# A doubling scan over 16 block sums, wider scan operations, a second buffer for the output tables and a new order of the chain's steps

## The chip, the cores and the metric

The kernel runs on one core of one Trainium2 chip. The metric is the device time of one execution in microseconds (us). The five engines of the core run their own queues in order: PE (matmul), DVE (vector), ACT (scalar), POOL (GpSimd) and SP, which here only issues DMAs. ACT issues DMAs too.

## The reference

One layer of a bidirectional hybrid encoder: 2048 tokens of width 1024, all in float32.

```
h = rms_norm(x);  [q | k | v | z_attn | u_ssm | z_ssm | gates] = h @ w_in
attn = windowed_gqa(q, k, v, sink, bias) * silu(z_attn)          # 8 heads, band of +-128
for each of 2 directions:                                        # 32 groups, 64 states each
    bu = u_group @ b_bar                                         # complex
    x[t] = a_bar * x[t-1] + bu[t]     (or backward)              # diagonal complex recurrence
    y += Re(c x)
y = gelu(y); y = y * sigmoid(y @ w_glu + b_glu); ssm = y * silu(z_ssm)
merged = sigmoid(g_attn) * (attn @ w_a) + sigmoid(g_ssm) * (ssm @ w_s)
out = rms_norm(x + merged @ w_out)
```

## The kernel before

Every large matmul is done as three (high part by high part, high by low, low by high), so each operand is split: ACT copies the high part, DVE or POOL subtracts it to get the low part. Weights arrive 128 columns at a time through SP into `raw` (two buffers); ACT writes `wh` (L164), POOL writes `wl` in four pieces (L156).

The program has one main order, a list of projections (`proj`: 24 matmuls of 512 columns into one of three `pj` banks, L221 to L223, then one evacuation by ACT). Beside it runs a side generator, `chain`: first the recurrence (`ssm`), then the attention, then preparations for the tail. After every six matmuls the main order grants the chain some credit (rate 1.237 per twelve matmuls while the recurrence runs), and the chain advances by one `yield` for each whole credit. So a step of the chain is a place in the order of every queue: what it issues stands there between the projections' instructions, on all engines. The order is written out by hand; nothing is moved by a planner, and an engine that waits holds up all that is queued behind it on that engine.

The recurrence works on 32 groups, four at a time (`GB = 4`), in eight rounds. T = 8 tokens are merged into one column, so M = 256 columns are scanned. A round i has these parts:

- `prep_w(i)` and `prep_o(i)`: POOL makes the input tables `wt` and the output tables `wo`, each by 24 TENSOR_TENSORs of 128x128 (L639 to L641).
- `load_u(i)`: four DMAs on SP bring the round's inputs into the tile `u` (one buffer). `split_u(i, half)` makes high and low parts of two groups (ACT `U0h`, `U1h` at L672; DVE `U0l`, `U1l` at L673); after half 1 the next round is loaded.
- `mats(i)`: PE transposes `wt` (L699), ACT and DVE make `Wh`, `Wl` (L702, L693).
- `inject(i)`: PE makes the scan's input (L756), ACT copies it into `X` (L757, L758).
- `zmat(i)`: `sign_o` changes the sign of `wo[1]` on ACT (L655), PE multiplies `wo` (L723, L730), DVE copies to `Z` (L731 to L733), and DMAs reorder it into `M`.
- `split_m(i)`, `split_o(i)`: high and low parts of `M` and of `wo` (`Mh`, `ws0h`, `ws1h` on ACT, `Ml`, `ws0l`, `ws1l` on DVE, all at L672, L673).
- `scan(i)`: all on DVE, in place in `X`: a tree of levels up (n = 128, 64, 32, ... 1 columns to update) and down (1, 3, 7, ... 127). With n > 32 a level is three SCALAR_TENSOR_TENSORs for each of the four groups (L774 to L776); with n up to 32 it is four TENSOR_TENSORs for all four groups at once (L786 to L789). Each call of `fma` yields an estimate of its cost, and a step of the chain (with one piece of `pieces()`) is taken each time the estimates add up to a slot.
- `hcopy(i, half)`: ACT copies two groups of `X` to `Hh` (L806), DVE makes `Hl` (L808), one buffer each. `emit(i, half)`: PE makes the output (L818, L822), ACT evacuates it (L826).

While `scan(i)` runs, `pieces()` of round i does the work of its neighbours: `mats(i+1)`, `emit(i-1)`, `inject(i+1)` and `zmat(i+1)`. `hcopy(i, 0)` comes after the last piece.

Of the kernel before, what the change touches and what calls it, by code (L numbers as in the profile page):

```python
# [7 lines left out]
F32 = mybir.dt.float32  # L8
# [17 lines left out]
GB = 4  # L26
# [12 lines left out]
def kernel(  # L39
# [381 lines left out]
    wo_im = prm.tile([128, G, T], F32, name="wo_im")  # L421
    NLEV = 8
    lv_re = prm.tile([128, G, NLEV], F32, name="lv_re")
    lv_im = prm.tile([128, G, NLEV], F32, name="lv_im")
    lv_ni = prm.tile([128, G, NLEV], F32, name="lv_ni")
    lv_sw = prm.tile([128, G, 2, NLEV], F32, name="lv_sw")
    bx_re = prm.tile([128, G + 1, C], F32, name="bx_re")
    bx_im = prm.tile([128, G + 1, C], F32, name="bx_im")
# [6 lines left out]
    def ssm_params(pool):  # L435
# [50 lines left out]
        def ts(o, a, s1, s2, o1, o2):  # L486
            if s2 is None:
                V.tensor_scalar(o, a, s1, None, o1)
            else:
                V.tensor_scalar(o, a, s1, s2, o1, o2)  # L490
            return o
# [100 lines left out]
            cmul(pw_re[:, :, i], pw_im[:, :, i], pw(i // 2), pw(i - i // 2))  # L592
        yield 8
        V.tensor_copy(lv_re[:, :, 0], pw_re[:, :, T])
        V.tensor_copy(lv_im[:, :, 0], pw_im[:, :, T])
        for i in range(1, NLEV):
            a = (lv_re[:, :, i - 1], lv_im[:, :, i - 1])
            cmul(lv_re[:, :, i], lv_im[:, :, i], a, a)
        ts(lv_ni, lv_im, -1.0, None, ALU.mult, None)
        V.tensor_copy(lv_sw[:, :, 0], lv_ni)  # L600
        V.tensor_copy(lv_sw[:, :, 1], lv_im)
        f, b_ = slice(0, 64), slice(64, 128)
        for dst_i, dst_o, src in ((wi_re, wo_re, pw_re), (wi_im, wo_im, pw_im)):
            V.tensor_copy(dst_i[f], src[f, :, 0:T])
# [16 lines left out]
    def ssm(pool):  # L621
# [9 lines left out]

        def table(i, tag, p_re, p_im, q_re, q_im, bufs):

            tmp = [pool.tile(sh, F32, tag=f"t{n}", name=f"t{n}") for n in range(2)]
            o = [pool.tile(sh, F32, tag=f"{tag}{n}", name=f"{tag}{n}", bufs=bufs) for n in range(2)]
            pr, pi, qr, qi = bc(p_re, i, 1), bc(p_im, i, 1), bc(q_re, i, 0), bc(q_im, i, 0)
            for n, (a, b, c, d, op) in enumerate(((pr, qr, pi, qi, ALU.subtract), (pr, qi, pi, qr, ALU.add))):
                for g in range(GB):
                    Q.tensor_tensor(tmp[0][:, g], a[:, g], b[:, g], ALU.mult)  # L639
                    Q.tensor_tensor(tmp[1][:, g], c[:, g], d[:, g], ALU.mult)  # L640
                    Q.tensor_tensor(o[n][:, g], tmp[0][:, g], tmp[1][:, g], op)  # L641
            return o

        def prep_w(i):
            st[i] = {"wt": table(i, "wt", wi_re, wi_im, bb_re, bb_im, 1)}

        def prep_o(i):
            st[i]["wo"] = table(i, "wo", wo_re, wo_im, cc_re, cc_im, 1)

        def split_o(i):  # L650
            st[i]["ws"] = [split(t, sh, f"ws{n}", 1) for n, t in enumerate(st[i].pop("wo"))]
# [9 lines left out]

            return bass.AP(tensor=t.tensor, offset=t.offset + g * C * T * M, ap=[[M, T], [T * M, C], [1, M]])

        def load_u(i):
            U = pool.tile([128, GB, M], F32, tag="u", name="u")
            for g in range(GB):
                nc.sync.dma_start(out=U[:, g], in_=chan(uS, i * GB + g))
            raw_u[i] = U

        def split(raw, shape, tag, bufs):  # L670
            hi, lo = [pool.tile(shape, F32R, tag=tag + t, name=tag + t, bufs=bufs) for t in "hl"]
# [2 lines left out]
            return hi, lo  # L674

        def split_u(i, half):
            u = raw_u[i][:, half * 2:half * 2 + 2]
            st[i].setdefault("U", []).append(split(u, [128, 2, M], f"U{half}", 2))
            if half == 1 and i + 1 < NB:
                load_u(i + 1)  # L680

        def split_m(i):
            st[i]["M"] = split(st[i].pop("m"), [128, GB, 128], "M", 1)
# [77 lines left out]
        def scan(i):  # L761

            g0 = i * GB
            X = st[i]["X"]

            def fma(dst, src, lev, n):

                if n > 32:
                    for g in range(GB):
                        d, s_ = X[:, g, :, dst], X[:, g, :, src]  # L770
                        re = lv_re[:, g0 + g, lev:lev + 1]
                        im = lv_im[:, g0 + g, lev:lev + 1]
                        ni = lv_ni[:, g0 + g, lev:lev + 1]
                        V.scalar_tensor_tensor(d, s_, re, d, ALU.mult, ALU.add)  # L774
                        V.scalar_tensor_tensor(d[:, 0], s_[:, 1], ni, d[:, 0], ALU.mult, ALU.add)
                        V.scalar_tensor_tensor(d[:, 1], s_[:, 0], im, d[:, 1], ALU.mult, ALU.add)  # L776
                        if g % 2 == 1:
                            yield 1.5 if n > 64 else 0.9
                else:
                    sh = [128, GB, 2, n]  # L780
                    t = pool.tile([128, GB, 2, 32], F32, tag="ft", name="ft", bufs=1)[:, :, :, 0:n]
                    u = pool.tile([128, GB, 2, 32], F32, tag="fu", name="fu", bufs=1)[:, :, :, 0:n]
                    d, s_ = X[:, :, :, dst], X[:, :, :, src]
                    re = lv_re[:, g0:g0 + GB, lev:lev + 1].unsqueeze(2).to_broadcast(sh)
                    sw = lv_sw[:, g0:g0 + GB, :, lev:lev + 1].to_broadcast(sh)
                    V.tensor_tensor(t, s_, re, ALU.mult)  # L786
                    V.tensor_tensor(u, s_[:, :, ::-1], sw, ALU.mult)
                    V.tensor_tensor(t, t, u, ALU.add)
                    V.tensor_tensor(d, d, t, ALU.add)  # L789
                    yield 0.25 + 4 * GB * 2 * n / 960.0  # L790

            for lev in range(NLEV):
                s_ = 1 << lev
                n = M // (2 * s_)
                yield from fma(slice(2 * s_, M + 1, 2 * s_), slice(s_, M + 1 - s_, 2 * s_), lev, n)
            for lev in range(NLEV - 2, -1, -1):
                s_ = 1 << lev
                n = M // (2 * s_) - 1
                yield from fma(slice(3 * s_, M + 1, 2 * s_), slice(2 * s_, M + 1 - s_, 2 * s_), lev, n)
# [31 lines left out]
                st.pop(i)  # L831

        prep_w(0)
        load_u(0)
        prep_o(0)
        for _ in range(7):
            yield
# [6 lines left out]
        for i in range(NB):  # L844

            def pieces():
                nx = i + 1 < NB
                if nx:
                    for _ in range(4 if i == 0 else 0):
                        yield  # L850
                    yield from mats(i + 1)
                    if i + 2 < NB:
                        prep_w(i + 2)
                if i > 0:
                    yield from emit(i - 1, 0)
                    hcopy(i - 1, 1)
                if nx:
                    split_u(i + 1, 0)
                if i > 0:
                    for _ in range(3):  # L860
                        yield
                    yield from emit(i - 1, 1)
                if nx:
                    split_u(i + 1, 1)
                split_m(i)
                split_o(i)
                if nx:
                    prep_o(i + 1)
                    for _ in range(2 if i == 0 else 0):
                        yield  # L870
                    yield from inject(i + 1)
                    yield from zmat(i + 1)

            pc = pieces()
            left = SCAN_SLOT * FIRST
            for c_ in scan(i):
                left -= c_
                if left <= 0:
                    next(pc, None)
                    yield  # L880
                    left += SCAN_SLOT
            for _ in pc:
                yield
            hcopy(i, 0)
# [747 lines left out]
```

## Time and profile before

| | before |
|---|---|
| time, median of 3 runs | 1542.53 us (1540.98 to 1546.22) |
| profiled execution: time / span | 1538.41 us / 1536.3 us |
| PE busy | 1426.9 us (93%) |
| DVE busy | 1047.8 us (68%) |
| ACT busy | 646.3 us (42%) |
| POOL busy | 593.8 us (39%) |
| granted clock of PE, mean | 0.971 |

The time is that of one whole execution, the span that from its first to its last instruction. [...] The durations in rows are those of single instructions; a wait stands in brackets behind an instruction, with what ended it.

### The profile page before, as it was taken

To read this page: it belongs to the slowest core of one execution; us is meant where nothing else is said; L and a number is where in the kernel's file an instruction comes from. 1 tells how busy PE (TensorE), PEld (TensorE's weight loads), DVE (VectorE), ACT (ScalarE), POOL (GpSimd) and SP (SyncE) were. 2 spreads that over 40 slices of the span, in tenths; PEclk is the share of its full clock that TensorE was granted. 3 is DMA by queue.
4 is the path that set the end of the run, shared out by engine and by line. 5 is a ranking of instruction groups with operands and counts; after the bars stand their busy time and mean duration, and the time that the engine had idled before them with its cause. 6 is when DMAs were issued, how large, how long until landed. Compare 5 with 4: busy or idle time off the path is not lost.

```text
span 1536.3 us, 20313 instructions
## 1 busy us (share of the span) xinstructions
PE 1426.9 (93%) x6933; PEld 1159.7 (75%) x6933; DVE 1047.8 (68%) x2371; ACT 646.3 (42%) x1165; POOL 593.8 (39%) x887
## 2 busy tenths in 40 slices
PE   7999999887898898989999999999989998999998
PEld 6787777776676677768888888888767786877886
DVE  3325729979779779765899998883577376386342
ACT  6332223424243344423666666664544143243111
POOL 5510368574655554623111111113268054153220
PEclk9999999998899999999999999999999999999999
DMA  7443232222232222427233333334676376375341
GB/s 262 152 120 92 74 100 83 86 73 78 91 100 69 93 93 83 137 86 213 83 97 96 97 96 97 94 92 131 202 202 183 126 190 179 103 186 185 114 125 69
DMA packets 240727, 185.51 MB, mean 121 GB/s; under 512 B 57920, under 2 KB 202432, under 8 KB 240624
## 3 DMA queue, kind: packets, MB, share of 16 engines
q10 hardware_dynamic: 108336, 100.61, 22.3%
q1 hardware_dynamic: 132288, 83.62, 18.3%
q8 instruction: 54, 0.88, 0.2%
q14 instruction: 49, 0.40, 0.1%
HBM read 126.56 MB, written 57.62 MB: 120 GB/s over the span
## 4 chain that ended last, share of the span: by engine, by line
PE 37%; DVE 27%; POOL 8%; DMA 6%; issue 6%; ACT 4%; ACTq 0%; DVEq 0%; POOLq 0%; SPq 0%
PE pj L221 7%; PE pj L223 7%; PE pj L222 7%; PE s L1478 3%; PE s L1479 3%; PE s L1480 3%; DVE Hl L808 2%; DVE X L774 2%; POOL t L639 2%; DMA yt<-yS 2%; PE s L1049 2%; POOL t L640 2%; POOL wo L641 2%; DVE X L776 2%; PE s L996 2%
## 5 line engine op out<-in xcount | busy, mean ns | idle before, releaser
L156 POOL TENSOR_TENSOR wl<-raw,wh 128x256 fp32r<-128x256 f32 x380 | 321.2, 876 | 592.5 <-ACT wh L164 450.5
L221 PE MATMUL pj<-hh,wh 128*128 128x512 f32 x976 | 397.6, 407 | 0.0
L223 PE MATMUL pj<-hh,wl 128*128 128x512 f32 x976 | 389.9, 400 | 7.3 <-POOL wl L156 7.3
L222 PE MATMUL pj<-hl,wh 128*128 128x512 f32 x976 | 389.6, 399 | 0.0
L223 PEld LDWEIGHTS pj<-hh,wl 128*128 128x128 f32 x976 | 188.0, 193 | 50.6 <-POOL wl L156 8.6
L221 PEld LDWEIGHTS pj<-hh,wh 128*128 128x128 f32 x976 | 189.0, 194 | 38.0 <-issue 4.1
L222 PEld LDWEIGHTS pj<-hl,wh 128*128 128x128 f32 x976 | 188.7, 193 | 34.3
L164 ACT ACTIVATE wh<-raw 128x1024 fp32r<-128x1024 f32 x96 | 100.7, 1051 | 18.6 <-issue 4.1
L1478 PE MATMUL s<-woh,mh 128*128 128x512 f32 x256 | 101.9, 398 | 6.7 <-DVE xr L1485 6.7
L1480 PE MATMUL s<-woh,ml 128*128 128x512 f32 x256 | 101.3, 396 | 0.0
L1479 PE MATMUL s<-wol,mh 128*128 128x512 f32 x256 | 101.2, 395 | 0.0
L405 ACT ACTIVATE st<-pj,bg 128x512 f32<-128x512 f32 x64 | 44.0, 687 | 120.4 <-PE pj L223 120.3
L774 DVE SCALAR_TENSOR_TENSOR X<-X,lv_re 128x256 f32<-128x256 f32 (+3 forms) x128 | 83.0, 648 | 0.3
L1013 ACT ACTIVATE p<-p,sml 128x384 f32<-128x384 f32 (+1 forms) x128 | 75.8, 594 | 16.4 <-DVE sml L1009 16.3
L997 DVE CUSTOM_DVE_ANT_0 p<-s,bias 128x384 f32<-128x384 f32 (+1 forms) x128 | 68.4, 535 | 14.4 <-PE s L996 14.1
L1522 POOL TENSOR_TENSOR sm<-sm,mhalf 128x1 f32<-128x1 f32 x15 | 8.3, 552 | 170.5 <-DVE sm L1521 133.9
L1485 DVE TENSOR_TENSOR xr<-xr,s 128x512 f32<-128x512 f32 x32 | 21.9, 685 | 68.6 <-PE s L1480 68.6
L1038 DVE TENSOR_TENSOR pl<-s,ph 128x512 fp32r<-128x512 f32 x92 | 62.9, 683 | 4.3 <-ACT ph L1036 2.9
L996 PE MATMUL s<-kst,qs 128*128 128x384 f32 (+1 forms) x256 | 65.7, 339 | 0.0
L776 DVE SCALAR_TENSOR_TENSOR X<-X,lv_im 128x128 f32<-128x128 f32 (+3 forms) x128 | 64.9, 507 | 0.0
L1478 PEld LDWEIGHTS s<-woh,mh 128*128 128x128 f32 x256 | 48.1, 188 | 20.7 <-DVE xr L1485 9.3
L641 POOL TENSOR_TENSOR wo<-t,t 128x128 f32<-128x128 f32 x64 | 31.8, 497 | 71.1 <-DVE ws0l L673 66.6
(279 smaller groups left out, 3027.4 us busy)
## 6 DMA issues: line engine op xcount, KB each, us to landing
raw<-in_w_in_dram SPq DMA_DIRECT2D x59, 512.0 KB
gS<-st ACTq DMA_DIRECT2D x64, 256.0 KB
gt<-gS ACTq DMA_DIRECT2D x64, 256.0 KB
x<-in_x_dram SPq DMA_DIRECT2D x16, 512.0 KB
raw<-in_w_branch_attn_dram SPq DMA_DIRECT2D x32, 256.0 KB
raw<-in_w_branch_ssm_dram SPq DMA_DIRECT2D x32, 256.0 KB
out_dram<-xr ACTq DMA_DIRECT2D x15, 512.0 KB
xr<-in_x_dram SPq DMA_DIRECT2D x12, 512.0 KB
```

The source lines that it names most:

```text
L156: eng.tensor_tensor(lo[:, ks], r[:, ks], hi[:, ks].bitcast(F32), ALU.subtract)
L164: A.activation(res[0], r, AF.Copy)
L221: PE.matmul(pt, w[0][:, k], r[0][:, k], start=start and k == 0, stop=False)
L222: PE.matmul(pt, w[0][:, k], r[1][:, k], start=False, stop=False)
L223: PE.matmul(pt, w[1][:, k], r[0][:, k], start=False, stop=stop and k == kt - 1)
L774: V.scalar_tensor_tensor(d, s_, re, d, ALU.mult, ALU.add)
L776: V.scalar_tensor_tensor(d[:, 1], s_[:, 0], im, d[:, 1], ALU.mult, ALU.add)
L996: PE.matmul(pt[:, 0:w], s["qs"][:, h], kst[:, r, kv, k0 * 128:k1 * 128], start=r == 0, stop=r == 1)
L1013: A.activation(p[:, h, 0:w], p[:, h, 0:w], AF.Exp, bias=nm[:, j:j + 1], accum_out=den[:, j:j + 1])
L1478: PE.matmul(pt, mh[k][:, ts_], wo[0, n][:, k], start=k == 0, stop=False)
L1479: PE.matmul(pt, mh[k][:, ts_], wo[1, n][:, k], start=False, stop=False)
L1480: PE.matmul(pt, ml[k][:, ts_], wo[0, n][:, k], start=False, stop=k == KD - 1)
```

## The change

Scan: the levels up and down with n = 64 and 63 take the form of four TENSOR_TENSORs for all groups (so `ft` and `fu` grow to 64 columns). The tree goes up and down over four levels only; in place of the levels n = 8, 4, 2, 1 up and 1, 3, 7 down, four doubling levels run over every 16th column (n = 15, 14, 12, 8). `lv_im` becomes a view of `lv_sw`, `lv_ni` is gone.

Tables: `wo` gets two buffers, and the temporaries of `table` are one group wide.

Inputs: `u` holds two groups instead of four, still in one buffer. `load_u(i, 1)` is issued right after `split_u(i, 0)`, `load_u(i+1, 0)` after `split_u(i, 1)`.

Order: in a round, `prep_o(i+1)` moves from behind `split_o(i)` to behind the first half of `mats(i+1)`; the second half of `mats(i+1)` comes after `emit(i-1, 0)` and `hcopy(i-1, 1)`; `prep_w(i+2)` moves behind `split_u(i+1, 0)`; one idle `yield` is left out.

```diff
--- before.py
+++ after.py
@@ -421,8 +421,6 @@
     wo_im = prm.tile([128, G, T], F32, name="wo_im")
     NLEV = 8
     lv_re = prm.tile([128, G, NLEV], F32, name="lv_re")
-    lv_im = prm.tile([128, G, NLEV], F32, name="lv_im")
-    lv_ni = prm.tile([128, G, NLEV], F32, name="lv_ni")
     lv_sw = prm.tile([128, G, 2, NLEV], F32, name="lv_sw")
     bx_re = prm.tile([128, G + 1, C], F32, name="bx_re")
     bx_im = prm.tile([128, G + 1, C], F32, name="bx_im")
@@ -592,13 +590,12 @@
             cmul(pw_re[:, :, i], pw_im[:, :, i], pw(i // 2), pw(i - i // 2))
         yield 8
         V.tensor_copy(lv_re[:, :, 0], pw_re[:, :, T])
+        lv_im = lv_sw[:, :, 1]
         V.tensor_copy(lv_im[:, :, 0], pw_im[:, :, T])
         for i in range(1, NLEV):
             a = (lv_re[:, :, i - 1], lv_im[:, :, i - 1])
             cmul(lv_re[:, :, i], lv_im[:, :, i], a, a)
-        ts(lv_ni, lv_im, -1.0, None, ALU.mult, None)
-        V.tensor_copy(lv_sw[:, :, 0], lv_ni)
-        V.tensor_copy(lv_sw[:, :, 1], lv_im)
+        ts(lv_sw[:, :, 0], lv_im, -1.0, None, ALU.mult, None)
         f, b_ = slice(0, 64), slice(64, 128)
         for dst_i, dst_o, src in ((wi_re, wo_re, pw_re), (wi_im, wo_im, pw_im)):
             V.tensor_copy(dst_i[f], src[f, :, 0:T])
@@ -631,21 +628,21 @@
 
         def table(i, tag, p_re, p_im, q_re, q_im, bufs):
 
-            tmp = [pool.tile(sh, F32, tag=f"t{n}", name=f"t{n}") for n in range(2)]
             o = [pool.tile(sh, F32, tag=f"{tag}{n}", name=f"{tag}{n}", bufs=bufs) for n in range(2)]
             pr, pi, qr, qi = bc(p_re, i, 1), bc(p_im, i, 1), bc(q_re, i, 0), bc(q_im, i, 0)
             for n, (a, b, c, d, op) in enumerate(((pr, qr, pi, qi, ALU.subtract), (pr, qi, pi, qr, ALU.add))):
                 for g in range(GB):
-                    Q.tensor_tensor(tmp[0][:, g], a[:, g], b[:, g], ALU.mult)
-                    Q.tensor_tensor(tmp[1][:, g], c[:, g], d[:, g], ALU.mult)
-                    Q.tensor_tensor(o[n][:, g], tmp[0][:, g], tmp[1][:, g], op)
+                    tmp = [pool.tile([128, T, C], F32, tag=f"t{m}", name=f"t{m}") for m in range(2)]
+                    Q.tensor_tensor(tmp[0], a[:, g], b[:, g], ALU.mult)
+                    Q.tensor_tensor(tmp[1], c[:, g], d[:, g], ALU.mult)
+                    Q.tensor_tensor(o[n][:, g], tmp[0], tmp[1], op)
             return o
 
         def prep_w(i):
             st[i] = {"wt": table(i, "wt", wi_re, wi_im, bb_re, bb_im, 1)}
 
         def prep_o(i):
-            st[i]["wo"] = table(i, "wo", wo_re, wo_im, cc_re, cc_im, 1)
+            st[i]["wo"] = table(i, "wo", wo_re, wo_im, cc_re, cc_im, 2)
 
         def split_o(i):
             st[i]["ws"] = [split(t, sh, f"ws{n}", 1) for n, t in enumerate(st[i].pop("wo"))]
@@ -661,11 +658,11 @@
 
             return bass.AP(tensor=t.tensor, offset=t.offset + g * C * T * M, ap=[[M, T], [T * M, C], [1, M]])
 
-        def load_u(i):
-            U = pool.tile([128, GB, M], F32, tag="u", name="u")
-            for g in range(GB):
-                nc.sync.dma_start(out=U[:, g], in_=chan(uS, i * GB + g))
-            raw_u[i] = U
+        def load_u(i, half):
+            U = pool.tile([128, 2, M], F32, tag="u", name="u")
+            for j in range(2):
+                nc.sync.dma_start(out=U[:, j], in_=chan(uS, i * GB + half * 2 + j))
+            raw_u[i, half] = U
 
         def split(raw, shape, tag, bufs):
             hi, lo = [pool.tile(shape, F32R, tag=tag + t, name=tag + t, bufs=bufs) for t in "hl"]
@@ -674,10 +671,12 @@
             return hi, lo
 
         def split_u(i, half):
-            u = raw_u[i][:, half * 2:half * 2 + 2]
+            u = raw_u.pop((i, half))
             st[i].setdefault("U", []).append(split(u, [128, 2, M], f"U{half}", 2))
-            if half == 1 and i + 1 < NB:
-                load_u(i + 1)
+            if half == 0:
+                load_u(i, 1)
+            elif i + 1 < NB:
+                load_u(i + 1, 0)
 
         def split_m(i):
             st[i]["M"] = split(st[i].pop("m"), [128, GB, 128], "M", 1)
@@ -765,21 +764,20 @@
 
             def fma(dst, src, lev, n):
 
-                if n > 32:
+                if n > 64:
                     for g in range(GB):
                         d, s_ = X[:, g, :, dst], X[:, g, :, src]
                         re = lv_re[:, g0 + g, lev:lev + 1]
-                        im = lv_im[:, g0 + g, lev:lev + 1]
-                        ni = lv_ni[:, g0 + g, lev:lev + 1]
+                        ni, im = (lv_sw[:, g0 + g, r, lev:lev + 1] for r in range(2))
                         V.scalar_tensor_tensor(d, s_, re, d, ALU.mult, ALU.add)
                         V.scalar_tensor_tensor(d[:, 0], s_[:, 1], ni, d[:, 0], ALU.mult, ALU.add)
                         V.scalar_tensor_tensor(d[:, 1], s_[:, 0], im, d[:, 1], ALU.mult, ALU.add)
                         if g % 2 == 1:
-                            yield 1.5 if n > 64 else 0.9
+                            yield 1.5
                 else:
                     sh = [128, GB, 2, n]
-                    t = pool.tile([128, GB, 2, 32], F32, tag="ft", name="ft", bufs=1)[:, :, :, 0:n]
-                    u = pool.tile([128, GB, 2, 32], F32, tag="fu", name="fu", bufs=1)[:, :, :, 0:n]
+                    t = pool.tile([128, GB, 2, 64], F32, tag="ft", name="ft", bufs=1)[:, :, :, 0:n]
+                    u = pool.tile([128, GB, 2, 64], F32, tag="fu", name="fu", bufs=1)[:, :, :, 0:n]
                     d, s_ = X[:, :, :, dst], X[:, :, :, src]
                     re = lv_re[:, g0:g0 + GB, lev:lev + 1].unsqueeze(2).to_broadcast(sh)
                     sw = lv_sw[:, g0:g0 + GB, :, lev:lev + 1].to_broadcast(sh)
@@ -789,11 +787,16 @@
                     V.tensor_tensor(d, d, t, ALU.add)
                     yield 0.25 + 4 * GB * 2 * n / 960.0
 
-            for lev in range(NLEV):
+            TREE = 4
+            for lev in range(TREE):
                 s_ = 1 << lev
                 n = M // (2 * s_)
                 yield from fma(slice(2 * s_, M + 1, 2 * s_), slice(s_, M + 1 - s_, 2 * s_), lev, n)
-            for lev in range(NLEV - 2, -1, -1):
+            b = 1 << TREE
+            for lev in range(TREE, NLEV):
+                s_ = 1 << lev
+                yield from fma(slice(b + s_, M + 1, b), slice(b, M + 1 - s_, b), lev, (M - s_) // b)
+            for lev in range(TREE - 1, -1, -1):
                 s_ = 1 << lev
                 n = M // (2 * s_) - 1
                 yield from fma(slice(3 * s_, M + 1, 2 * s_), slice(2 * s_, M + 1 - s_, 2 * s_), lev, n)
@@ -831,7 +834,7 @@
                 st.pop(i)
 
         prep_w(0)
-        load_u(0)
+        load_u(0, 0)
         prep_o(0)
         for _ in range(7):
             yield
@@ -848,16 +851,20 @@
                 if nx:
                     for _ in range(4 if i == 0 else 0):
                         yield
-                    yield from mats(i + 1)
-                    if i + 2 < NB:
-                        prep_w(i + 2)
+                    ms = mats(i + 1)
+                    next(ms)
+                    prep_o(i + 1)
+                    yield
                 if i > 0:
                     yield from emit(i - 1, 0)
                     hcopy(i - 1, 1)
                 if nx:
+                    yield from ms
                     split_u(i + 1, 0)
+                    if i + 2 < NB:
+                        prep_w(i + 2)
                 if i > 0:
-                    for _ in range(3):
+                    for _ in range(2 if nx else 3):
                         yield
                     yield from emit(i - 1, 1)
                 if nx:
@@ -865,7 +872,6 @@
                 split_m(i)
                 split_o(i)
                 if nx:
-                    prep_o(i + 1)
                     for _ in range(2 if i == 0 else 0):
                         yield
                     yield from inject(i + 1)
```

## Rows read from the trace of the kernel before

**Rows 1.** Busy time by stretch: PE, PEld, DVE, ACT, POOL, granted clock, DMA share, GB/s

```profile
220.00:686.00 466.00, 406.31 (x2174) 332.81 (x2174) 389.86 (x865) 176.40 (x257) 257.43 (x441) 0.92 0.29 91
686.00:1100.00 414.00, 411.13 (x2039) 342.25 (x2037) 325.85 (x917) 250.04 (x580) 75.31 (x96) 1.00 0.39 115
1440.00:1460.00 20.00, 20.00 (x87) 16.06 (x86) 11.02 (x16) 6.13 (x8) 10.97 (x13) 1.00 0.61 160
```

**Rows 2.** Waits of PE: who waited for whom, total, times, longest

```profile
PE s L822 <- DVE Hl L808: 31.3, 7, 6.3
PE s L723 <- ACT wo L655: 17.8, 6, 4.4
PE pj L223 <- POOL wl L156: 10.6, 5, 3.7
```

**Rows 3.** Busy time, as in Rows 1, of four short stretches

```profile
317.60:324.40 6.80, 4.66 (x18) 3.46 (x19) 4.45 (x8) 1.38 (x3) 4.43 (x7) 0.50 0.12 26
382.46:385.87 3.41, 3.41 (x16) 2.68 (x9) 0.77 (x2) 1.48 (x2) 3.41 (x6) 0.50 0.22 82
556.50:563.40 6.90, 5.66 (x20) 3.99 (x20) 2.24 (x4) 0.78 (x2) 3.49 (x5) 0.51 0.37 116
614.60:621.40 6.80, 5.86 (x20) 4.00 (x20) 1.12 (x3) 2.67 (x4) 4.97 (x8) 0.50 0.24 75
```

**Rows 4.** Costliest groups: the output tables on POOL

```profile
L641 POOL TENSOR_TENSOR wo<-t,t 128x128 f32<-128x128 f32 x64 | 31.8, 497 | 71.1 <-DVE ws0l L673 66.6
```

**Rows 5.** Timeline of DVE in one round: start, duration, instruction

```profile
392.74 2.62 DVE L808 TENSOR_TENSOR Hl<-X,Hh 64x1024 fp32r<-64x1024 f32 x2 [2.67 <-ACT Hh L806]
...
401.27 0.59 DVE L774 SCALAR_TENSOR_TENSOR X<-X,lv_re 128x128 f32<-128x128 f32 x1
...
409.25 0.63 DVE L786 TENSOR_TENSOR ft<-X,lv_re 128x256 f32<-128x256 f32 x1
...
413.79 3.39 DVE L808 TENSOR_TENSOR Hl<-X,Hh 64x1024 fp32r<-64x1024 f32 x2
...
417.92 0.42 DVE L786 TENSOR_TENSOR ft<-X,lv_re 128x64 f32<-128x64 f32 x1
...
423.87 0.37 DVE L786 TENSOR_TENSOR ft<-X,lv_re 128x120 f32<-128x120 f32 x1
...
425.27 0.66 DVE L786 TENSOR_TENSOR ft<-X,lv_re 128x248 f32<-128x248 f32 x1
...
427.52 0.70 DVE L673 TENSOR_TENSOR U1l<-u,U1h 128x512 fp32r<-128x512 f32 x1
...
445.32 0.27 DVE L731 COPY Z<-s 128x112 f32<-128x112 f32 x1 [2.92 <-PE s L723]
```

**Rows 6.** Timeline of DVE in the first round, where POOL is idle

```profile
224.73 0.45 DVE L774 SCALAR_TENSOR_TENSOR X<-X,lv_re 128x128 f32<-128x128 f32 x1
...
228.72 0.67 DVE L786 TENSOR_TENSOR ft<-X,lv_re 128x256 f32<-128x256 f32 x1
```

**Rows 7.** Timeline of PE where that round's low parts come

```profile
417.24 0.58 PE L822 MATMUL s<-Hl,ws0h 128*128 128x256 f32 x1 [6.27 <-DVE Hl L808]
```

**Rows 8.** Timeline of SP, start of the recurrence; "x2" is two DMAs and the wait between

```profile
181.60 21.70 SPq L184 DMA_DIRECT2D raw<-in_w_in_dram  x2
203.91 0.60 SPq L667 DMA_DIRECT2D u<-uS  x1
...
220.64 0.36 SPq L734 DMA_DIRECT2D zS<-Z  x1
...
223.44 0.60 SPq L738 DMA_DIRECT2D M<-zS  x1
```

**Rows 9.** Timeline of ACT and of PE in the same stretch

```profile
186.04 0.62 ACT L672 ACTIVATE U1h<-u 128x512 fp32r<-128x512 f32 x1
186.56 0.59 ACT L702 ACTIVATE Wh<-s 128x512 fp32r<-128x512 f32 x1
...
194.36 0.41 PE L756 MATMUL s<-U0h,Wh 128*128 128x256 f32 x1
```

## The prediction, on record before the changed kernel ran

> **What bounds the kernel now.** I read the busy time by stretch first. From 686 to 1100 us PE is busy 411 of 414 us at full clock: nothing is to be gained there. From 220 to 686 us, the recurrence, it is busy 406 of 466 us, at a mean clock of 0.92; DVE is busy 390 us and POOL 257 us [rows 1]. So some 60 us of PE's idle time, and its low clock, lie where this change works. The amount of matmul work doesn't change, so I keep the books by PE: the time changes by what PE waits more or less, and by what the low clock costs after a wait.
>
> The waits of PE name the two causes: 31.3 us in seven waits for `Hl` (L808) at the second half of `emit`, and 17.8 us in six waits for `wo` from ACT (L655) at `zmat` [rows 2]. The second goes back to POOL. It stood 66.6 us of idle time before the output tables, for DVE's `ws0l` [rows 4]: one buffer of `wo`, so `prep_o(i+1)` can't write before `split_o(i)` has read, and `sign_o` and `zmat(i+1)` then wait for the table. Behind the longer of these waits the clock falls to 0.50: four stretches of 6.8, 3.4, 6.9 and 6.8 us [rows 3], where PE loses half, 12 us.
>
> The DVE timeline of one round shows the other cause. From `Hl(i, 0)` at 392.74 to the end of `Hl(i-1, 1)` at 417.18, 24.4 us, DVE works without a gap through the levels n = 128, 64, 32 and 16 [rows 5]. PE arrives 6.27 us too early [rows 7]. I call these 24.4 us the first stretch. After it PE sets the pace, and DVE waits for PE before `Z` at 445.32 [rows 5]. So an instruction saved on DVE counts in the first stretch and hardly in the second.
>
> **Second buffer and early `prep_o`.** The table no longer waits for `split_o`. It is 24 instructions of 0.50 us [rows 4], 12 us, issued twelve steps ahead of `sign_o`. A step is 12 / 1.237 = 9.7 matmuls; 87 matmuls took 20 us [rows 1], so it is 2.2 us of PE, and twelve are 27 us. The table is ready, and the six waits go with their low clock: 17.8 + 12.0 = **-29.8 us**. If POOL were behind by more than 15 us, nothing of it would come.
>
> **Scan.** Four TENSOR_TENSORs took 1.40 us at n = 15 and 2.25 us at n = 31 [rows 5], so +0.85 us for 16 columns, and at n = 63 by extension 3.95 us. The twelve instructions that they replace took 3.99 us with POOL idle [rows 6], but 7.98 us beside POOL's work, of which some 1.3 us are two `Wl` in between [rows 5]: 6.7. Bounds for the wide form: four dense 128x512 at 0.70 us [rows 5], 2.8, and all the slowing that the narrow form has, 3.95 x 6.7 / 3.99 = 6.6. POOL slowed twelve instructions by 2.7 us; for four I take somewhat more than a third, 1.5: 5.5 us, a gain of 1.2 in the first stretch. The seven middle levels took 5.95 us (417.92 to 423.87) [rows 5]; the four new ones, three near 1.4 and one near 1.1, cost 5.2. Both this and n = 63 lie in the second stretch, where PE paces: nothing, except in the last round, where PE only waits for DVE: 1.2 + 1.2 + 0.8, **-3 us**.
>
> [...]
>
> **Order.** Between `Hl(i, 0)` and the `Hl`-matmul of `emit(i-1, 1)` there is now one step less, so PE arrives 2.2 us earlier; DVE has the two `Wl` behind it instead of in front, 1.3 us, and 1.2 from n = 64. That is -2.5 + 2.2: the wait stays. Bounds: POOL runs ahead and its table falls into DVE's idle time (-4 us a round), or `prep_w`, now just behind, slows the levels n = 32 and 16 too (+3). In the one middle round that doesn't wait today, a step earlier starts a wait: 2.2 us and half of a 3.4 us low stretch, **+4 us**. The left-out step itself only moves 2.2 us of projections behind the recurrence. The two parameter copies and the narrower temporaries cost and gain nothing that shows: they lie on DVE before the tables and in POOL's order.
>
> **Half a tile of inputs.** `u` still has one buffer, so the load of half 1 can't be queued before `split_u(i, 0)`, and `split_u(i, 1)` needs it. In round 0 both stand side by side. Today ACT runs `U1h` at 186.04, then `Wh`, and PE's first `inject` matmul starts at 194.36 [rows 9]. In SP's queue the load would take the place where the next round's load is now, 203.91, behind a weight load that hangs until POOL's two tables and the `wl` behind them are done [rows 8]. Its second DMA goes out 0.65 us later and lands 2.8 us after that (as `zS` to `M`, 220.64 to 223.44 [rows 8]): 207.4. Queued behind `U1h` on ACT are both `Wh` and the evacuations, and for `Wh` and `Wl` waits PE: 207.4 + 0.5 + 0.6 + 0.6 + 0.7, about 209.5. PE idles 15 us; in exchange the wait for `wl` of 3.7 us that lies in this stretch [rows 2] is covered, and the clock behind costs about 1 us more: **+12 us**. Bounds: 0, if something lets the load pass the weight load, and 17.
>
> In later rounds four steps, 8.8 us, lie between the halves, and the load takes 1.2 + 2.8 = 4.0: nothing, with 4.8 us to spare. If a weight load in front hangs on a 12 us table, 7 us a round are missing, 43 in six.
>
> **Sum.** 1538.4 (the profiled execution's own time) - 29.8 - 3 + 4 + 12 = 1521.6. The median of the runs shown is 4.1 us above the profiled time, so I say **1526 us**. Without rivals I'd give 1512 to 1540.
>
> **Rivals.**
> First, more gain: the first stretch shrinks by 4 us in five rounds, because `prep_o` waits for nobody and is done before DVE starts on n = 128: 1526 - 20 = 1506. For it speaks that level 64 costs 4.0 us beside an idle POOL and 6.7 beside a busy one [rows 5, 6]; against it, that `prep_w` and the weights' `wl` come right after.
>
> Second, the other side: the second input half is late in every round. ACT stands at `U1h`, DVE at `U1l`, and the evacuations and the scan behind them. The price is up to 7 us a round; with 5 us in six rounds 1526 + 30 = 1556, slower than before. It decides when SP's load goes out more than 4.8 us after its turn, because a weight load hangs in front of it. For it: the 21.7 us for which SP hung at the start [rows 8]. Against it: `prep_w` is issued behind the load, so only older POOL work can hold it up.
>
> Third, the change does nothing that counts: the six `wo` waits go, but PE then stands at `Hl`, because it arrives 2.2 us earlier and DVE is slowed by two tables in a row, some 1 us more. 3.2 us in five rounds are 16: 1542. For it: DVE was already the later one seven times [rows 2]. Against it: fewer instructions on DVE in that stretch. [...]
>
> **Chances.** Forecast 0.45, more gain 0.17, late half 0.18, nothing that counts 0.20. What this kernel's measurement can tell from no change is 0.3%, 4.6 us. Of the forecast I count 0.38 as faster, 0.05 same, 0.02 slower; more gain all as faster; late half 0.02 same, 0.16 slower; nothing that counts 0.03 faster, 0.13 same, 0.04 slower. Together 0.58, 0.20, 0.22. The range reaches from below the first rival to the second: 1500 to 1556.
>
> **What the profile would show.** Right: no wait of L723 on ACT, none of POOL on `ws0l`, seven or eight waits on `Hl` of about the same length, one hole in PE of some 15 us before the first L756 with ACT waiting for a DMA at `U1h`. Wrong: later waits at `U1h` or of L756 (second rival), waits on `Hl` of 8 us and more (third), below 3 us (first), or new waits for `wl` because two tables follow each other on POOL.

## The result, and the profile after

The changed kernel takes 1529.49 us (median of 4 runs, 1525.99 to 1530.28), the kernel before 1541.76 us in the runs beside it. The ratio is 0.992, its 95% interval 0.9895 to 0.9945: faster by 0.55 to 1.05%. The forecast was 1526 us. The profiled execution has a span of 1528.5 us.

The recurrence first, by the busy time in the same 466 us (columns as in [rows 1]):

```profile
220.00:686.00 466.00, 423.31 (x2338) 346.81 (x2337) 385.10 (x649) 185.16 (x272) 300.51 (x450) 0.96 0.33 101
```

PE does 17 us more in this stretch than before, at a granted clock (a share of the full one) of 0.96 in place of 0.92. DVE has a quarter fewer instructions and is busy almost as long; POOL is busy 43 us longer [rows 1]. The stretch holds somewhat more of the rounds than before, so this isn't all POOL's slowing; the experiments separate that.

PE's waits (total, times, longest) answer to [rows 2], and the group of the output tables on POOL to [rows 4]:

```profile
PE s L825 <- DVE Hl L811: 26.8, 10, 5.2
PE s L755 <- ACT Wh L701: 17.5, 1, 17.5
...
PE pj L223 <- POOL wl L156: 8.0, 4, 3.1
```

```profile
L638 POOL TENSOR_TENSOR wo<-t,t 128x128 f32<-128x128 f32 x64 | 34.5, 539 | 5.0
```

The 17.8 us of waits for `wo` are gone, and POOL no longer stands 66.6 us for `ws0l`. In their place stands one wait of 17.5 us. Its story is in the timelines of SP, ACT and PE at the start of the recurrence, which answer to [rows 8] and [rows 9]:

```profile
181.14 24.10 SPq L184 DMA_DIRECT2D raw<-in_w_in_dram  x2
205.83 7.53 SPq L664 DMA_DIRECT2D u<-uS  x4
```

```profile
210.57 0.63 ACT L669 ACTIVATE U1h<-u 128x512 fp32r<-128x512 f32 x1 [22.96 <-DMA u<-uS]
...
211.11 1.07 ACT L701 ACTIVATE Wh<-s 128x512 fp32r<-128x512 f32 x2
```

```profile
211.74 0.58 PE L755 MATMUL s<-U0h,Wh 128*128 128x256 f32 x1 [17.49 <-ACT Wh L701]
```

The second half of round 0's inputs goes out at 205.83, behind the weight load (it is the first two of the four DMAs, the others are round 1's first half). ACT stands 22.96 us at `U1h`, `Wh` stands behind it in ACT's queue, and PE behind `Wh`.

One round on DVE, in the place of [rows 5]:

```profile
394.22 3.29 DVE L811 TENSOR_TENSOR Hl<-X,Hh 64x1024 fp32r<-64x1024 f32 x2 [1.77 <-ACT Hh L809]
...
403.73 1.23 DVE L784 TENSOR_TENSOR ft<-X,lv_re 128x512 f32<-128x512 f32 x1
404.87 1.16 DVE L785 TENSOR_TENSOR fu<-X,lv_sw 128x512 f32<-128x512 f32 x1
406.06 0.74 DVE L786 TENSOR_TENSOR ft<-ft,fu 128x512 f32<-128x512 f32 x1
406.83 1.24 DVE L787 TENSOR_TENSOR X<-X,ft 128x512 f32<-128x512 f32 x1
...
410.74 0.38 DVE L784 TENSOR_TENSOR ft<-X,lv_re 128x128 f32<-128x128 f32 x1
...
412.36 2.60 DVE L811 TENSOR_TENSOR Hl<-X,Hh 64x1024 fp32r<-64x1024 f32 x2
414.99 0.69 DVE L692 TENSOR_TENSOR Wl<-s,Wh 128x512 fp32r<-128x512 f32 x1
```

From `Hl(i,0)` to the end of `Hl(i-1,1)` are now 20.7 us, 24.4 before [rows 5]. The wide level takes 4.34 us (403.73 to 408.07). The row at 410.74 matters later: the level n = 16 lies in front of `Hl(i-1,1)`. PE waits less at the same place, but waits [rows 7]; and the sixth round, which had no such wait before, now has one:

```profile
415.01 0.58 PE L825 MATMUL s<-Hl,ws0h 128*128 128x256 f32 x1 [3.62 <-DVE Hl L811]
...
569.47 0.39 PE L825 MATMUL s<-Hl,ws0h 128*128 128x256 f32 x1 [2.54 <-DVE Hl L811]
```

### The profile page after: what moved, and what is told of

The parts are those of the page before. It is cut to its first block, busy times and chain, and to the rows that moved or that the text cites. A ratio compares the mean times of both kernels' runs of the same rounds, so it can differ in the third digit from the quotient of the medians.

```text
span 1528.5 us, 20091 instructions
## 1 busy us (share of the span) xinstructions
PE 1423.8 (93%) x6933; PEld 1154.0 (75%) x6933; DVE 1027.4 (67%) x2145; ACT 644.7 (42%) x1165; POOL 629.1 (41%) x887
## 4 chain that ended last, share of the span: by engine, by line
PE 46%; DVE 19%; DMA 8%; POOL 6%; issue 5%; ACT 4%; ACTq 0%; SPq 0%; POOLq 0%; DVEq 0%
PE pj L221 9%; PE pj L223 9%; PE pj L222 9%; DVE Hl L811 3%; PE s L1484 3%; PE s L1485 3%; PE s L1486 3%; PE s L1055 2%; PE s L1002 2%; PE s L1039 2%; DMA yt<-yS 2%; POOL wl L156 2%; DMA ar<-aS 2%; DVE ft L784 1%; DVE fu L785 1%
## 5 line engine op out<-in xcount | busy, mean ns | idle before, releaser
L156 POOL TENSOR_TENSOR wl<-raw,wh 128x256 fp32r<-128x256 f32 x380 | 329.8, 899 | 597.8 <-ACT wh L164 586.2
L1042 ACT ACTIVATE ph<-s 128x512 fp32r<-128x512 f32 x92 | 54.3, 590 | 57.5 <-PE s L1039 57.5
L1044 DVE TENSOR_TENSOR pl<-s,ph 128x512 fp32r<-128x512 f32 x92 | 63.2, 687 | 19.2 <-ACT ph L1042 17.8
L1002 PE MATMUL s<-kst,qs 128*128 128x384 f32 (+1 forms) x256 | 61.7, 342 | 0.6 <-issue 0.6
L1039 PE MATMUL s<-ident,p 128*128 128x128 f32 x368 | 57.6, 274 | 0.0
L1039 PEld LDWEIGHTS s<-ident,p 128*128 128x128 f32 x368 | 46.4, 140 | 14.7 <-DVE p L1031 2.2
```

The costliest lines, as they stand in the source:

```text
L156: eng.tensor_tensor(lo[:, ks], r[:, ks], hi[:, ks].bitcast(F32), ALU.subtract)
L1002: PE.matmul(pt[:, 0:w], s["qs"][:, h], kst[:, r, kv, k0 * 128:k1 * 128], start=r == 0, stop=r == 1)
L1039: PE.transpose(pt[:, h * 128:(h + 1) * 128], s["p"][:, h, i * 128:(i + 1) * 128], ident)
```

## The experiments

Times are medians; ratios are to the kernel before, run beside each, with 95% intervals. The intervals are 2.5 to 6.4 us to each side, so two kernels that are less than some 5 us apart are called alike. Theory: the tables and their low clock give the gain, round 0's half tile takes half of it back, the scan counts for little. Rivals: the half tile costs every round; the tables' gain went into new waits at `Hl`; the scan itself gives or costs.

**1. Half tiles of inputs alone, on the kernel before.**

```diff
-            U = pool.tile([128, GB, M], F32, tag="u", name="u")
+            U = pool.tile([128, 2, M], F32, tag="u", name="u")
...
+            if half == 0:
+                load_u(i, 1)
```

> The kernel before with the half tile of inputs alone. Theory: it costs one hole in PE at the start of the recurrence, about 17 us with ACT waiting for the input DMA at U1h, less the 3.7 us wait for wl that it covers: +12 to +16 us, 1554 to 1558, and no wait of PE on U1l above 3 us in later rounds. Rival (the second half is late in every round): +30 us or more, 1572, with several later waits.

Measured: 1556.6 us, ratio 1.0104 (1.0063 to 1.0145), +14.7 us. PE's waits show the hole, by itself and once:

```profile
PE s L758 <- ACT Wh L704: 16.5, 1, 16.5
```

**2. Early tables alone, on the kernel before.** To make room, the two temporaries of the tables become one, a group wide (the first product goes into the table itself), and one buffer of `ncc` is dropped.

```diff
-            st[i]["wo"] = table(i, "wo", wo_re, wo_im, cc_re, cc_im, 1)
+            st[i]["wo"] = table(i, "wo", wo_re, wo_im, cc_re, cc_im, 2)
...
-                    yield from mats(i + 1)
+                    ms = mats(i + 1)
+                    next(ms)
+                    prep_o(i + 1)
+                    yield
+                    yield from ms
```

> The kernel before with two buffers of wo and prep_o(i+1) behind the first half of mats(i+1), nothing else of the order or the scan; to make room one temporary of the tables and one buffer of ncc go. Theory: the six waits of PE on wo and the low clock behind four of them go, -30 us, 1512. Rival (PE only reaches the Hl wait earlier): the Hl waits grow by about as much as the wo waits lose, 1535 to 1542.

Measured: 1517.73 us, ratio 0.9848 (0.982 to 0.9875), -24.0 us. PE no longer waits for `wo`. The waits that are left:

```profile
PE s L822 <- DVE Hl L808: 32.1, 8, 6.6
PE pj L223 <- POOL wl L156: 11.3, 5, 5.1
...
PE s L756 <- DVE U1l L673: 4.9, 2, 2.7
```

Those for `Hl` and `wl` are as in [rows 2]: the gain wasn't lost there. 0.8 and 0.7 us of it are missing in them, 2.7 at `U1l`, for which PE waited 2.2 us before. By the pages of the profiled executions PE's idle time (the span less its busy time) fell from 109.4 to 99.4 us, and its busy time for the same 6933 matmuls from 1426.9 to 1417.9: the first is waits, the second clock (0.978 on average in place of 0.971).

**3. The changed kernel with whole input tiles.** The same two savings of memory as in 2.

```diff
-            U = pool.tile([128, 2, M], F32, tag="u", name="u")
+            U = pool.tile([128, GB, M], F32, tag="u", name="u")
```

> The changed kernel with the inputs loaded whole as before (four groups in one tile); one temporary of the tables and one buffer of ncc go to make room. Theory: the hole of 17.5 us in PE at the start goes, the 3.7 us wait for wl comes back: -12 to -16 us against the changed kernel, 1514 to 1518. Rival (the time at the start was hidden, since the first scan had to wait for zmat anyway): same as the changed kernel, 1529.

Measured: 1513.01 us, ratio 0.9814 (0.9784 to 0.9843), 16.5 us less than the changed kernel. The hole is gone; in exchange the waits for `wl` double, which the hole had covered:

```profile
PE pj L223 <- POOL wl L156: 16.6, 7, 6.0
```

By the pages PE's whole idle time is 90.3 us, 14.4 less than in the changed kernel.

**4. Half tiles, but round 0's second half loaded at the start** into `M`'s buffer, which is free then.

```diff
-            U = pool.tile([128, 2, M], F32, tag="u", name="u")
+            U = pool.tile([128, 2, M], F32, tag="M" if (i, half) == (0, 1) else "u", name="u")
...
-            if half == 0:
+            if half == 0 and i > 0:
```

> The changed kernel, but round 0 loads its second input half at the start into the buffer of M, which is free then; all later rounds load half by half as in the changed kernel. Theory: the half tile costs time in round 0 alone. The hole of 17.5 us in PE goes, the time is that of the variant with whole inputs, 1511 to 1517 us. Rival: the later rounds pay too (waits at U1l and behind them): 1518 to 1524 us. If the hole was only hidden idle time that comes back elsewhere (waits for wl): above 1524 us.

Measured: 1516.77 us, ratio 0.9844 (0.9813 to 0.9874), 12.7 us less than the changed kernel. All later rounds still load by halves, and ACT still stands for them:

```profile
ACT U1h L669 <- DMA u<-uS: 14.5, 5, 7.7
```

So round 0 is the place, and the savings of memory in 3, which this run does without, are not what gained there. The 3.8 us to variant 3 are within the intervals; whether the later halves cost anything isn't settled.

**5. The new scan alone, on the kernel before.** The scan and the `lv_im` view, nothing else.

```diff
-                if n > 32:
+                if n > 64:
...
+            TREE = 4
+            for lev in range(TREE, NLEV):
```

> The kernel before with the new scan alone (levels of 64 and 63 wide, doubling over 16 sums). Theory: DVE works 2 to 3 us less in each round, but the rounds are paced by wo and PE in their second stretch; only the first stretch (1 us) and the last round (3 us) count: -3 to -10 us, 1532 to 1539. Rival (the scan is where the gain of the change comes from): -20 us or more, below 1522.

Measured: 1551.23 us, ratio 1.0067 (1.0041 to 1.0094): 9.3 us slower. The expectation missed. PE's waits, the output tables on POOL, and the busy time:

```profile
PE s L823 <- DVE Hl L809: 35.5, 9, 6.3
PE s L720 <- ACT wo L652: 23.6, 6, 5.8
PE pj L223 <- POOL wl L156: 14.4, 4, 6.1
```

```profile
L638 POOL TENSOR_TENSOR wo<-t,t 128x128 f32<-128x128 f32 x64 | 34.0, 531 | 51.0 <-DVE ws0l L670 46.4
```

```profile
220.00:686.00 466.00, 400.56 (x2146) 326.35 (x2145) 362.12 (x640) 172.76 (x252) 292.71 (x441) 0.92 0.28 89
```

DVE is busy 28 us less than in [rows 1]. POOL executes the same number of instructions (x441) and takes 35 us longer for them, and one instruction of the tables takes 531 ns in place of 497 [rows 4]. Beside the wide DVE instructions POOL is slower. Both what POOL makes (`wo`, `wl`) and `Hl` come later: these three kinds of wait have grown by 5.8, 3.8 and 4.2 us [rows 2].

**6. Only the wide form of n = 64 and 63, on the kernel before**: as 5, but the tree goes over all levels.

> The kernel before with only the levels n = 64 and 63 in the wide form; the tree goes over all levels as before. It tells apart why the new scan alone was 9.3 us slower. Theory: the wide instructions hold POOL off, the output tables come later and the waits for wo grow: 1546 to 1556 us, output tables of 13 us, waits for wo over 21 us. Rival: the four doubling levels did it, since with them a round has fewer steps for the same pieces: the wide form alone gives 1537 to 1544 us.

Measured: 1547.64 us, ratio 1.0043 (1.0026 to 1.006), +7.3 us. One instruction of the tables takes 600 ns, and PE's waits for `wo` are those of 5:

```profile
L638 POOL TENSOR_TENSOR wo<-t,t 128x128 f32<-128x128 f32 x64 | 38.4, 600 | 46.3 <-DVE ws0l L670 41.7
```

```profile
PE s L720 <- ACT wo L652: 22.7, 6, 5.9
```

The wide form does most of it, not the doubling levels; the 3.6 us between 5 and 6 are within the intervals. POOL's instructions in one round, and DVE's beside the last two of them, show where the time goes:

```profile
407.54 0.58 POOL L637 TENSOR_TENSOR t<-wi_im,bx_re 128x128 f32<-128x128 f32 x1
...
409.03 1.12 POOL L637 TENSOR_TENSOR t<-wi_im,bx_re 128x128 f32<-128x128 f32 x1
410.22 1.06 POOL L638 TENSOR_TENSOR wt<-t,t 128x128 f32<-128x128 f32 x1
```

```profile
408.84 1.09 DVE L782 TENSOR_TENSOR ft<-X,lv_re 128x512 f32<-128x512 f32 x1
409.85 1.16 DVE L783 TENSOR_TENSOR fu<-X,lv_sw 128x512 f32<-128x512 f32 x1
```

The same POOL operation takes 0.58 us beside the narrow instructions of n = 128 and 1.12 beside the wide level. I sorted this trace's table instructions from 220 to 686 us by what DVE ran longest beside them: the 51 beside a wide instruction take 1.00 us on average, the 112 beside SCALAR_TENSOR_TENSORs of the scan 0.49.

**7. The changed kernel with the old scan.**

```diff
-                if n > 64:
+                if n > 32:
...
-            for lev in range(TREE):
+            for lev in range(NLEV):
```

> The change with the old scan (n = 64 and 63 group by group, the tree over all levels); order, buffers and half inputs as in the changed kernel. Theory: the new scan was dear on the kernel before only because the output tables stood on the path there and the wide instructions slow POOL; with the tables issued early that costs nothing, and the 4 us a round less on DVE shorten the waits for Hl. So without it: 1535 to 1543 us, waits for Hl 35 to 42 us in place of 26.8. Rival: the new scan is a loss here too, or does nothing: 1518 to 1530 us, waits for Hl not above 30 us.

Measured: 1526.78 us, ratio 0.9912 (0.9886 to 0.9937): as the changed kernel. The rival was right: here too the new scan gives nothing. PE's waits for `Hl` are even shorter, and the DVE timeline of the same round shows why:

```profile
PE s L820 <- DVE Hl L806: 23.6, 11, 4.0
```

```profile
395.26 3.29 DVE L806 TENSOR_TENSOR Hl<-X,Hh 64x1024 fp32r<-64x1024 f32 x2 [1.77 <-ACT Hh L804]
...
404.66 0.72 DVE L772 SCALAR_TENSOR_TENSOR X<-X,lv_re 128x128 f32<-128x128 f32 x1
...
410.08 0.49 DVE L774 SCALAR_TENSOR_TENSOR X<-X,lv_sw 128x64 f32<-128x64 f32 x1
...
413.14 2.71 DVE L806 TENSOR_TENSOR Hl<-X,Hh 64x1024 fp32r<-64x1024 f32 x2
...
416.49 0.36 DVE L784 TENSOR_TENSOR ft<-X,lv_re 128x128 f32<-128x128 f32 x1
```

The narrow level n = 64 takes 5.9 us (404.66 to 410.57), so the wide one saves 1.6. But here the level n = 16 (416.49) stands behind `Hl(i-1,1)`, in the changed kernel in front of it, for 1.6 us (410.74 to 412.36). The steps of the chain are placed by the estimates that `fma` yields, but at each yield at most one step is taken. For the wide level `fma` yields once (2.4, from 0.25 + 4 x 512 / 960), for the narrow one twice (0.9 each), so the wide level has room for one step where the narrow one has room for two, and the step with `Hl(i-1,1)` falls a level later. From `Hl(i,0)` to the end of `Hl(i-1,1)` it is 20.6 us, against 20.7. POOL is busy 274.0 us from 220 to 686 us, 26.5 less than beside the new scan in the same order.

**8. The changed kernel with `prep_o` late again**, behind `split_o`; the second buffer stays.

```diff
-                    prep_o(i + 1)
                     yield
...
                 split_o(i)
                 if nx:
+                    prep_o(i + 1)
```

> The changed kernel with prep_o back behind split_o; the second buffer of wo stays. Theory: both are needed. Five steps, some 11 us, lie between this place and sign_o, and the table takes 13 us on POOL and has the weights' low parts in its queue: PE waits for wo some 3 us a round again and the clock falls behind it, 1537 to 1550 us. Rival: the buffer does it all, since POOL only stood because of split_o: no wait for wo above 1 us, 1525 to 1533 us.

Measured: 1543.29 us, ratio 1.002 (1.0004 to 1.0036), 13.8 us more than the changed kernel. PE waits for `wo` again:

```profile
PE s L722 <- ACT wo L652: 15.8, 3, 6.5
```

The second buffer alone is not enough. At the late place POOL starts one round's table at 315 us and ends it at 331, and PE waits 3.4 us for it until 331.6; in the changed kernel a table of that stretch begins at 282 and is done at 295. The table needs the early place as well.

**9. The idle step put back**, in the changed kernel.

```diff
-                    for _ in range(2 if nx else 3):
+                    for _ in range(3):
```

> The changed kernel with the left-out step put back: three idle yields in place of two between hcopy(i-1,1) and emit(i-1,1). Theory: the step less is why the waits for Hl stayed; with it PE comes 2.2 us later and the waits of 3.5 us in five or six rounds fall to about 1.3: -11 to -13 us and a little of the low clock, 1513 to 1520 us. Rival: PE then waits as long elsewhere (U1l, X, wl), or the projections run out behind the recurrence: 1525 to 1533 us.

Measured: 1518.8 us, ratio 0.9837 (0.9795 to 0.9878), -10.7 us against the changed kernel. The waits for `Hl` fall by 11.3 us:

```profile
PE s L825 <- DVE Hl L811: 15.5, 13, 2.2
...
PE s L755 <- DVE U1l L670: 4.6, 4, 2.3
```

The rival was half right about the waits, and wrong about the time. New ones at `U1l` (4.6 us) have come, and those for `wl` are 3.3 us longer; by the pages PE's idle time fell only by 5.8 us. Another 4.5 us come from its busy time: with shorter waits the mean granted clock rose from 0.975 to 0.981.

**10. FIRST = 0.1 in place of 1.711**, in the changed kernel. FIRST is the share of a slot of scan estimates that must add up before the first piece of a round is taken.

```diff
-FIRST = 1.711
+FIRST = 0.1
```

> The changed kernel with FIRST = 0.1 in place of 1.711: the first piece of a round is taken one to two scan levels earlier, so Hl(i-1,1) stands that much earlier in DVE's queue, while PE's order of steps stays. Theory: DVE's queue in front of Hl sets the waits; they fall by 3 us and more each, the sum of them from 26.8 to under 10 us, 1508 to 1518 us. Rival: what is moved on DVE is only exchanged (Wl, U0l and Z come later behind the same levels): 1524 to 1533 us.

Measured: 1515.86 us, ratio 0.9818 (0.9783 to 0.9853), -13.6 us. The waits for `Hl` halve, if not quite to the sum expected. DVE's order of instructions in front of `Hl` sets them:

```profile
PE s L825 <- DVE Hl L811: 12.8, 10, 2.1
```

**11. Whole input tiles and the old scan**, with the changed kernel's tables and order.

> Whole input tiles, the changed kernel's order and second buffer, and the old scan. Theory after the run with the old scan: on this order the new scan neither gives nor costs, since DVE's shorter work and POOL's slower tables cancel; so as the variant with whole inputs and the new scan, 1508 to 1517 us. Rival: there the new scan is worth its 4 us a round: 1520 us and more.

Measured: 1511.15 us, ratio 0.979 (0.9755 to 0.9825): as variant 3 with the new scan (1513.01). The second pair that shows no worth in the new scan.

**12. What the runs point to, together.** As 11, with the step put back, FIRST = 0.1, and five idle yields in place of two between the last `hcopy(NB-1,0)` and the last `emit`.

> What the runs point to, together: the second buffer of wo and the early tables, whole input tiles, the old scan, FIRST = 0.1, three idle yields before emit(i-1,1), and five idle yields in place of two between the last hcopy and the last emit, where PE waits 6 us for Hh and runs at the low clock behind it. Theory: each takes away a wait of its own: 1511 (whole inputs with the old scan) - 13 (FIRST) - 2 (what the step still can) - 6 (end of the recurrence) = 1487 to 1498 us, waits for Hl under 8 us in all. Rival: once PE no longer waits for Hl, DVE is late elsewhere (U1l, Z, Wl) and half of the 21 us comes back: 1499 to 1508 us. At 1509 us and more the gains don't add.

Measured: 1496.18 us (median of 5), ratio 0.9702 (0.9678 to 0.9726): 45 us less than before, 33 less than the changed kernel. The recurrence's stretch, and PE's waits there:

```profile
220.00:686.00 466.00, 438.61 (x2414) 360.88 (x2413) 413.14 (x887) 194.52 (x282) 286.44 (x460) 0.99 0.36 111
```

```profile
PE s L696 <- DVE Z L728: 12.0, 5, 3.9
PE pj L223 <- POOL wl L156: 11.6, 6, 3.5
...
PE s L753 <- DVE U1l L670: 5.3, 4, 2.6
...
PE s L818 <- DVE Hl L804: 3.5, 3, 2.0
```

PE is busy 438.6 of 466 us at a clock of 0.99. Of the waits for `Hl` 3.5 us are left. 12 us of new ones have come, of the next round's transposes (L696) for DVE's copies to `Z`, whose source shares the banks `s2` with them: a part of DVE's lateness has moved to the next place where PE needs it.

## Why the prediction came out as it did

The forecast was 1526, the time 1529.5. Four steps lead from before to after through runs 2, 11 and 3; each difference carries some 5 us of uncertainty, and the last also brings the changed kernel's temporaries and `ncc` buffers back: early tables 1541.8 to 1517.7 (-24), the rest of the new order, on the old scan, to 1511.2 (-6.6), the new scan to 1513.0 (+1.9, not to be told from nothing), half tiles to 1529.5 (+16.5). Together -12.3, where the prediction summed -16.8. That the sum came out so near is in part luck: by this chain the tables gained 5.8 us less than forecast and the scan 4.9 less, the half tiles cost 4.5 more, and the order gained 10.6 more.

**Second buffer and early `prep_o`: -29.8 forecast, -24 measured.** The six waits are gone as said, and in the changed kernel no wait of `zmat` on `wo` is left. The term was some 6 us too large. In the place of the 17.8 us of waits PE finds small ones at `U1l`, `Hl` and `wl`, and its idle time fell by 10.0 (run 2). And the 12.0 us for the low clock were a slip: half of the four stretches' length, where PE was busy only 19.6 of the 23.9 us [rows 3], so the clock could give back 9.8; the busy time fell by 9.0. The step "the table is ready" was right, but depends on the place in the order: run 8 loses 13.8 us with the same buffers.

**Half a tile: +12 forecast, +14.7 alone and +16.5 in the whole.** The mechanism was right in each link, SP, ACT, PE. The hole was 17.5 us in place of 15, since ACT got the data at 210.57, 3.2 us later than the forecast load at 207.4. It covers `wl` waits as said, but more than the 3.7 us: 8.0 are left with it, 16.6 without. Other waits take most of that back, so that PE's idle time grows by 14.4 us (run 3). The second rival (every round) fell: with round 0 repaired, 12.7 us come back. Its sign came all the same. The load of later rounds was to have 4.8 us to spare, but ACT stands for it five times more, 14.1 us beside round 0's 23.0:

```profile
ACT U1h L669 <- DMA u<-uS: 37.1, 6, 23.0
```

PE has no wait for `U1l` in the changed kernel, and what these waits of ACT cost doesn't stand out: the 3.8 us between runs 3 and 4 are within the intervals.

**Scan: -3 forecast, +1.9 measured; the reasoning failed.** The wide level was priced at 5.5 us and took 4.34 (3.9 to 5.1 in the eight rounds); its gain in the first stretch, put at 1.2 us, was 1.6. The middle levels were said to cost 5.2 us in place of 5.95; in the round shown the four new ones take 6.4 (from 415.60 and from 418.60 us on). What the prediction left out were two effects. The wide level's single yield moved the chain's step a level later, so the gain went to the level n = 16, and `Hl` comes no earlier (run 7). And the wide instructions slow POOL (1.00 us for an instruction of the tables beside them, 0.49 beside narrow ones, run 6): the prediction only let POOL slow DVE. On the kernel before, where the tables lay on PE's path, that cost 7 to 9 us (runs 5 and 6); with the tables early neither pair of runs shows a cost or a gain. The -3 of the last round is not there. The prediction priced the level n = 64 with a busy POOL, but in the last round POOL is idle during it (from 592.7 to 613.0 us in the changed kernel), and there the wide form (605.70 to 609.64, changed kernel) takes as long as the narrow one (606.80 to 610.71, run 7):

```profile
605.70 1.07 DVE L784 TENSOR_TENSOR ft<-X,lv_re 128x512 f32<-128x512 f32 x1
...
607.79 0.69 DVE L786 TENSOR_TENSOR ft<-ft,fu 128x512 f32<-128x512 f32 x1
...
609.64 0.65 DVE L784 TENSOR_TENSOR ft<-X,lv_re 128x256 f32<-128x256 f32 x1
```

```profile
606.80 0.44 DVE L772 SCALAR_TENSOR_TENSOR X<-X,lv_re 128x128 f32<-128x128 f32 x1
...
610.71 2.46 DVE L806 TENSOR_TENSOR Hl<-X,Hh 64x1024 fp32r<-64x1024 f32 x2
```

PE's wait for the last `Hh` is 6.05 us in the changed kernel and 5.92 in run 7.

In averages over a run, one instruction of the output tables takes 497 ns before [rows 4], 531 and 600 ns in runs 5 and 6. Why a wide instruction slows POOL, no run shows.

**Order: +4 forecast, -6.6 measured; "the wait stays" was half right.** The wait stays, and fell more than the 0.3 us a round that was said: at the place of [rows 7] from 6.27 to 3.62 us, and from run 2 to run 11 the sum of these waits from 32.1 to 23.5. They are ten in the changed kernel, of 0.5 to 5.2 us, not seven or eight of one length. The first stretch shrank by 3.7 us (24.4 to 20.7) and not by 2.5. The step less was sized rightly at 2.2 us a round, as run 9 shows: with it back, the `Hl` waits fall by 11.3 us in all. The sentence that leaving it out only moves projections was the wrong way to see it: it is worth 10.7 us, and lay open in the prediction's own terms.

**The sixth round:** a new wait was forecast at 2.2 us plus low clock, 4 in all; it is 2.54 us at 569.47, and the clock is at 1.00 from 565 to 590 us.

The third rival (nothing that counts, since PE then stands at `Hl`) fell as a whole with run 2: those waits stayed as they were. But the earlier PE that it named was real and cost 10.7 us (run 9); the rest of the order gave more. The first rival's measure nearly came, 3.7 of its 4 us in the round shown, but not by its cause: the level n = 128 is no faster (395.36 to 401.27 before [rows 5], 397.51 to 403.73 now), and the stretch shrank at n = 64 and by the two `Wl` that left it.

## What to carry to other kernels

When steps of one queue are placed by cost estimates between the pieces of another, a piece that is faster or comes in fewer parts can move the steps: look at what now stands in front of the instruction that PE waits for, before counting the time saved. A buffer that is split to make room for another must be asked who waits for its second half in the first round, where both halves stand side by side. And a wait at an in-order engine has two cheap cures besides faster work: the producer's instruction earlier in its queue (13.6 us here), or the consumer one step later among work that is there anyway (10.7 us); each was measured alone.

## What was not expected of the hardware

A DVE form with a third of the instructions made POOL slower, not faster: in run 5, 441 POOL instructions in the same 466 us took 292.7 us in place of 257.4 [rows 1], and in run 6 a table instruction took twice as long beside a wide one as beside a narrow one (1.00 us against 0.49). The slow operations of the wide form are those that read or write strided slices of `X`: 1.16 to 1.24 us for 128x512, against 0.74 us for the one between `ft` and `fu` alone. POOL is not the reason: with POOL idle, in the last round, they take 1.07 to 1.09 us, against 0.69.
